# Differential attention in a two-layer decoder trunk: one written order of steps for all compute engines

## The chip, the cores and the metric

The kernel runs on one core of one Trainium2 chip. The core has a matrix engine (TensorE, PE in the profile; its weight loads are shown apart as PEld), a vector engine (VectorE, DVE), a scalar engine for activations (ScalarE, ACT), a general engine (GpSimd, POOL) and a queue engine (SyncE, SP) that starts most DMA transfers. Each engine works through its own list of instructions in order and waits for the others by semaphores. The metric is the device time of one execution in microseconds (us); less is better.

## What is computed

The reference is a trunk of two layers on 512 tokens of width 1024 in float32. Layer 0 runs latent attention (MLA) and differential attention side by side behind one input projection, concatenates the heads and projects back; layer 1 does the same with two other kinds of attention. Behind each layer stands a gated feed-forward block with a short convolution. The part that matters here is the differential attention of layer 0: four heads, each with two queries and two keys of width 64 and a value of width 128.

```
def diff_attention(q1, q2, k1, k2, v, lam, slopes):
    ...
        def probs(qb, kf):
            s = jnp.einsum('bhqd,bhkd->bhqk', qb, kf).astype(jnp.float32) * scale + bias
            return jax.nn.softmax(jnp.where(causal, s, -jnp.inf), axis=-1)

        p = probs(a1, k1) - lam * probs(a2, k2)
        return jnp.einsum('bhqk,bhkd->bhqd', p.astype(v.dtype), v)
...
    o_diff = rms_norm(o_diff, subln_g) * (1.0 - lam_init)
    return jnp.concatenate([heads_last(o_mla), heads_last(o_diff)], axis=-1) @ w_out
```

## The kernel before

Tokens are cut into four row blocks of 128, taken in the order 3, 2, 1, 0 (`ORDER`). Every projection is done with split operands: a weight tile and an activation tile are each held as a high and a low part, and `mm3` makes three matmuls of the pair (high x high, high x low, low x high). Here such a matmul is called a projection step; three of them are one k-tile of 128 rows. Weights arrive by DMA from SP's queue into three raw buffers (`wraw`) and are split by ACT (line 72, the high part `wh`) and DVE (line 73, the low part `wl`) into five pairs of buffers. The class `Weights` keeps the list of units and prepares some (`depth`) ahead of the one that is used.

The stage in question follows MLA. Its work is cut into 16 units, one for each head `h` and row block `i`, of `(i + 1) * 128` keys, since the attention is causal. A unit goes through these functions:

- `score`: two matmuls into two PSUM banks `s` (`sps`, line 844), for z = 0 (q1 k1) and z = 1 (q2 k2); then for each, on DVE, the sum with the ALiBi table and its minimum in one instruction (line 610) and, on ACT, the exponential with its row sum (line 614). DVE then takes the reciprocal of the second row sum (line 855), works out the factor from it, `st1` and `neglam` (line 856), adds the two probability tiles (line 857), and takes the reciprocal of the first row sum (line 858), which scales the output later.
- `turn`: PE transposes the tile block by block (`tpp`, line 621) into the single bank `t`, which ACT (odd row blocks) or DVE (even row blocks) copies out (`pt`, lines 624 and 626).
- `value`: PE multiplies by the value tile `dv` into the single bank `o` (line 869), DVE scales the result (line 871), ACT squares it with a row sum (line 873), POOL makes the inverse root (lines 178 and 181, in `rstd`).
- `norm`: DVE scales the row with that root and the gain `subg` (line 880). `finish`, once a head: four transposes (`tpo`, line 887) and the split into `oD`.

Two kinds of work fill PE in between. `diff_qk` projects queries (`aqk`, evicted by ACT) or keys (evicted by DVE) of heads 1 to 3, eight k-tiles each and six calls in all. `project(i, half, part)` is the output projection of a row block and one half of its columns into `ao`: part 0 takes the MLA outputs (`omh`, `oml`), part 1 those of this stage (`odh`, `odl`), four k-tiles each. `skewed` hands one whole call of these out at every second unit. The eight weight tiles of the output projection (`wout`) come from a small second list `W2` (the first three; two of them are prepared ahead of the units) and from the main list.

PE, ACT, DVE and POOL run in an order that a scheduler works out from this program; `score` asks it for high priority and ties the two scores to the release of both banks (`reads`). Behind the units stands a part whose order is written out by hand (`tc.manual_schedule`): the rest of the output projection, the post-norm, the residual sum and the pre-norm of the feed-forward block, with transposes of the normalised rows (`tp`, line 211). The feed-forward block of layer 0 follows.

Of the kernel before, what the change touches and what calls it, by code (L numbers as in the profile page):

```python
# [17 lines left out]
P = 128  # L18
# [68 lines left out]
def trunk(tc, A, out):  # L87
# [3 lines left out]
    with ExitStack() as top:  # L91
# [498 lines left out]
        def even():  # L590
            with ExitStack() as es:
# [14 lines left out]
                def softmax_negated(sc, ps, table, n, bufs, reads=None):  # L606

                    s = sc.tile([P, S], F32, tag="s", name="s", bufs=bufs)
                    st = sc.tile([P, 2], F32, tag="st", name="st", bufs=6)
# [204 lines left out]
                DVE.tensor_scalar(subg[:], subg[:], 1.0 - LAM_INIT, None, ALU.mult)  # L814
# [13 lines left out]
                wout = [W2.next() for _ in range(2)]  # L828
                nx = new_xnT()

                otoks, dens = {}, {}

                def score(h, i):
                    def f(_):
                        w = (i + 1) * P
                        if i == ORDER[0]:
                            otoks[h] = sc.tile([P, NT, P], F32, tag="otok", name="otok2", bufs=2)
                            dens[h] = sc.tile([P, 6, NT], F32, tag="den", name="den", bufs=2)
                        s_ps = [bank("s", "sps") for _ in range(2)]

                        with tc.high_priority():
                            for z in range(2):
                                r = slice(z * 64, (z + 1) * 64)
                                m = PE.matmul(s_ps[z][:, :w], dq[h][r, i * P:(i + 1) * P], dk[h][r, :w],
                                              start=True, stop=True)
                                if z:
                                    tc.keep_in_program_order(m)
                                else:
                                    for n in reads:
                                        tc.add_manual_dep(m.ins, n, SYNC, reason="both banks")  # L850
                        reads.clear()
                        (s2, st2), (s1, st1) = [softmax_negated(sc, s_ps[z][:, :w], alibi[:, h, 384 - i * P:], w, 5, reads)
                                                for z in (1, 0)]
                        v = dens[h][:, :, i:i + 1]
# [7 lines left out]
                def turn(h, i):  # L862
                    return lambda s: transposed(sc, s, i + 1, i % 2, "t")
# [46 lines left out]
                for h in range(4):  # L910
                    for i in ORDER:
                        st = [score(h, i), turn(h, i), value(h, i), norm(h, i)]
                        if i == ORDER[-1]:
                            st.append(finish(h))
# [508 lines left out]
```

## Time and profile before

| | |
|---|---|
| median of 3 runs | 1164.73 us (1162.73 to 1166.18) |
| the profiled execution | 1163.55 us |
| its span, first to last instruction | 1161.8 us |
| granted TensorE clock, mean | 0.996 |
| instructions | 15175 |
| transferred by DMA | 126.81 MB |

The profile shows one execution. Its page gives the busy time of each engine, a strip of 40 time slices, and groups of instructions by source line. A group says what is written and read by the program's names, the count, the total busy time, the mean of one in ns, and how long the engine was idle ahead of it and for whom. A timeline row gives a start, a duration, engine, line, operation, names, shape and count; `[1.56 <-DVE s L857]` at its end means idle time and who ended it. A window row gives, for a stretch of time, its length and each engine's busy time with the number of instructions, then the granted clock of TensorE, the share of time in which DMA engines were busy, and GB/s. Matmuls of the same engine overlap in the rows, so the pace of PE is read from one start to the next. The float32 matmuls of scores and value products (those without split operands) appear as two records each.

### The profile page before, as it was taken

The numbers are of one execution on the slowest core, as the hardware profiler recorded it, in microseconds if no ns is written. First come the engines' busy times: TensorE is split into PE (matmuls) and PEld (weight loads), VectorE is DVE, ScalarE is ACT, GpSimd is POOL, SyncE is SP. The second block draws the span as 40 slices with busy tenths as digits, with TensorE's granted clock in tenths as the row PEclk, the third lists the DMA queues.
The fourth block names the chain that finished last, engine by engine and source line by source line (L and its number), as shares of the span: only waits on it lengthen the run. The fifth ranks groups of instructions, "written<-read, shape, count | busy, mean of one in ns | idle before, by whom it ended". The sixth has DMA issues, their size and how long they took to land. (4 is left out here: it accounts for less than half of the span.)

```text
span 1161.8 us, 15175 instructions
## 1 busy us (share of the span) xinstructions
PE 1143.3 (98%) x5656; PEld 940.0 (81%) x5656; DVE 810.8 (70%) x1424; ACT 557.9 (48%) x942; POOL 57.0 (5%) x138
## 2 busy tenths in 40 slices
PE   8999999999999999999999999999999999999997
PEld 7876667898888888888888877898988888888885
DVE  6677676467766766899874465577676666679895
ACT  5565555245434434456543454545443443445562
POOL 2100012110000000000030000002000000000001
PEclk9999999999999999999999999999999999999999
DMA  7310521034333332355826213222233333324461
GB/s 278 121 64 1 170 73 37 37 130 128 93 104 93 94 105 84 100 156 162 251 93 177 73 55 93 92 73 94 91 109 96 104 91 97 103 82 145 145 200 73
DMA packets 39049, 126.81 MB, mean 109 GB/s; under 512 B 4672, under 2 KB 6336, under 8 KB 38848
## 3 DMA queue, kind: packets, MB, share of 16 engines
q1 hardware_dynamic: 37056, 122.11, 33.5%
q10 hardware_dynamic: 1920, 3.74, 1.1%
q8 instruction: 44, 0.72, 0.3%
q14 instruction: 29, 0.24, 0.1%
HBM read 117.95 MB, written 6.29 MB: 107 GB/s over the span
## 5 line engine op out<-in xcount | busy, mean ns | idle before, releaser
L73 DVE TENSOR_TENSOR wl<-wraw,wh 128x1024 fp32r<-128x1024 f32 (+1 forms) x202 | 244.4, 1218 | 181.1 <-ACT wh L72 180.9
L72 ACT CAST wh<-wraw 128x1024 fp32r<-128x1024 f32 (+1 forms) x202 | 209.5, 1046 | 282.8 <-PE u L264 179.4
L263 PE MATMUL u<-xh,wh 128*128 128x512 f32 (+1 forms) x768 | 285.0, 372 | 0.9 <-ACT xh L171 0.9
L264 PE MATMUL u<-xl,wh 128*128 128x512 f32 (+1 forms) x768 | 285.2, 372 | 0.1
L265 PE MATMUL u<-xh,wl 128*128 128x512 f32 (+1 forms) x768 | 285.1, 371 | 0.0
L263 PEld LDWEIGHTS u<-xh,wh 128*128 128x128 f32 x768 | 144.5, 188 | 26.3 <-ACT xh L171 1.3
L264 PEld LDWEIGHTS u<-xl,wh 128*128 128x128 f32 x768 | 144.7, 188 | 25.1 <-DVE xl L172 0.3
L265 PEld LDWEIGHTS u<-xh,wl 128*128 128x128 f32 x768 | 144.7, 188 | 24.8
L265 PE MATMUL acc<-wh,gl 128*128 128x512 f32 x248 | 96.5, 389 | 0.0
L264 PE MATMUL acc<-wl,gh 128*128 128x512 f32 x248 | 96.5, 389 | 0.0
L263 PE MATMUL acc<-wh,gh 128*128 128x512 f32 x248 | 96.4, 390 | 0.0
L417 ACT ACTIVATE y<-y 128x512 f32<-128x512 f32 x44 | 27.7, 632 | 85.1 <-DVE y L415 85.1
L412 ACT ACTIVATE y<-u,cw 128x512 f32<-128x512 f32 x88 | 67.4, 773 | 1.7 <-PE u L265 1.7
L415 DVE SCALAR_TENSOR_TENSOR y<-u,cw,y 128x510 f32<-128x510 f32 x88 | 65.6, 747 | 2.5
L413 DVE SCALAR_TENSOR_TENSOR y<-u,cw,y 128x511 f32<-128x511 f32 x88 | 65.1, 743 | 0.9 <-ACT y L412 0.9
L178 POOL TENSOR_TENSOR rv<-ms,epst 128x1 f32<-128x1 f32 x40 | 10.5, 263 | 913.7 <-ACT junk L230 841.4
L263 PEld LDWEIGHTS acc<-wh,gh 128*128 128x128 f32 x248 | 46.6, 188 | 10.2 <-issue 0.6
L265 PEld LDWEIGHTS acc<-wh,gl 128*128 128x128 f32 x248 | 46.6, 188 | 9.8
L264 PEld LDWEIGHTS acc<-wl,gh 128*128 128x128 f32 x248 | 46.6, 188 | 9.5
L263 PE MATMUL apt<-xh,wh 128*128 128x512 f32 x128 | 50.6, 395 | 0.0
L264 PE MATMUL apt<-xl,wh 128*128 128x512 f32 x128 | 50.0, 391 | 0.0
L265 PE MATMUL apt<-xh,wl 128*128 128x512 f32 x128 | 49.9, 390 | 0.0
(298 smaller groups left out, 1905.7 us busy)
## 6 DMA issues: line engine op xcount, KB each, us to landing
wraw<-in_ffn_w_up SPq DMA_DIRECT2D x88, 512.0 KB, 3.6
wraw<-in_ffn_w_down SPq DMA_DIRECT2D x44, 512.0 KB, 3.7
wraw<-in_od_w_dqk SPq DMA_DIRECT2D x12, 512.0 KB, 3.7
wraw<-in_ffn_w_down SPq DMA_DIRECT2D x22, 256.0 KB, 2.7
wraw<-in_ev_w_dqk SPq DMA_DIRECT2D x8, 512.0 KB, 4.0
wraw<-in_ev_w_out SPq DMA_DIRECT2D x8, 512.0 KB, 3.6
spill<-X SPq DMA_DIRECT2D x8, 512.0 KB, 2.6
X<-spill SPq DMA_DIRECT2D x8, 512.0 KB, 6.3
```

The lines of the kernel that those rows point to most:

```text
L72: self.nc.scalar.copy(h[:, :w], raw[:, :w])
L73: self.nc.vector.tensor_tensor(l[:, :w], raw[:, :w], h[:, :w].bitcast(F32), ALU.subtract)
L178: POOL.tensor_tensor(v[:, :n], ms, epst[:, :n], ALU.add)
L263: PE.matmul(o, lh, rh, start=first, stop=False, skip_group_check=more)
L264: PE.matmul(o, lh, rl, start=False, stop=False, skip_group_check=more)
L265: PE.matmul(o, ll, rh, start=False, stop=last, skip_group_check=more)
L412: ACT.activation(y[:, z], u, AF.Identity, bias=c[:, 3:4], scale=c[:, 2:3])
L413: DVE.scalar_tensor_tensor(y[:, z, 1:], u[:, :S - 1], c[:, 1:2], y[:, z, 1:], ALU.mult, ALU.add)
L415: DVE.scalar_tensor_tensor(y[:, z, 2:], u[:, :S - 2], c[:, 0:1], y[:, z, 2:], ALU.mult, ALU.add)
L417: ACT.activation(y[:, 0], y[:, 0], AF.Silu)
```

## The change

The 16 units are no longer handed to `skewed`. A loop over 20 steps, inside `tc.manual_schedule` for PE, DVE, ACT and POOL, writes out which part of which unit comes at which step: the two scores of unit n with their minima; a weight unit prepared (from `W2` at steps 3, 6 and 9); the exponentials of unit n; some filler; the transposes of unit n-1; the value product of unit n-2; more filler; the norm of unit n-3; the combination of unit n; and, every fourth step, `finish`. The filler is now cut into chunks of one k-tile: `plan` gives their number ahead of the transposes and behind the value product, mostly two and two (six projection steps each time). The two halves of row block 1 join the early output projections (`early`). All copies of transposed tiles, and the scaling of the value product, go to ACT. A unit's small columns (minima, sums, reciprocals, row sum of squares) stand in one tile `st` of eight columns; the two reciprocals become one instruction of two columns. The factor of the row mean of squares moves into the gain (`P ** 0.5`) and the epsilon column (`epsp`). No `wout` unit is prepared ahead of the loop, and the main list is prepared by explicit calls inside it (`W.depth` is 0 there), so SP's queue holds the six `ev_w_dqk` loads of heads 1 to 3 ahead of the eight `ev_w_out` loads, where two of the latter stood between.

```diff
@@ -811,7 +812,9 @@
                 ld = sc.tile([P, 1], F32, tag="ld", name="ld")
                 DVE.tensor_tensor(ld[:], le[:, 1:2], le[:, 0:1], ALU.subtract)
                 DVE.tensor_scalar(neglam[:], ld[:], -LAM_INIT, None, ALU.add)
-                DVE.tensor_scalar(subg[:], subg[:], 1.0 - LAM_INIT, None, ALU.mult)
+                DVE.tensor_scalar(subg[:], subg[:], (1.0 - LAM_INIT) * P ** 0.5, None, ALU.mult)
+                epsp = sc.tile([P, 1], F32, tag="epsp", name="epsp")
+                POOL.memset(epsp[:], P * EPS)
...
-                wout = [W2.next() for _ in range(2)]
+                wout = []
                 nx = new_xnT()
 
-                otoks, dens = {}, {}
+                otoks = {}
 
                 def score(h, i):
...
+                    if i == ORDER[0]:
+                        otoks[h] = sc.tile([P, NT, P], F32, tag="otok", name="otok2", bufs=2)
+                    w = (i + 1) * P
+                    ps = [bank("s", "sps")[:, :w] for _ in range(2)]
+                    for z in range(2):
+                        r = slice(z * 64, (z + 1) * 64)
+                        PE.matmul(ps[z], dq[h][r, i * P:(i + 1) * P], dk[h][r, :w], start=True, stop=True)
+                    st = sc.tile([P, 8], F32, tag="st", name="st", bufs=11)
+                    e = [sc.tile([P, S], F32, tag="s", name="s", bufs=5)[:, :w] for _ in range(2)]
+                    for z in range(2):
+                        DVE.tensor_tensor_reduce(out=e[z], in0=ps[z], in1=alibi[:, h, 384 - i * P:], scale=1.0,
+                                                 scalar=3e38, op0=ALU.add, op1=ALU.min, accum_out=st[:, 1 - z:2 - z])
+                    return e, st
+
+                def exps(a):
+                    e, st = a
+                    for z in range(2):
+                        ACT.activation(e[z], e[z], AF.Exp, bias=st[:, 1 - z:2 - z], scale=-1.0,
+                                       accum_out=st[:, 3 - z:4 - z])
+
+                def combine(a):
+                    e, st = a
+                    DVE.reciprocal(st[:, 4:6], st[:, 2:4])
+                    DVE.scalar_tensor_tensor(st[:, 6:7], st[:, 4:5], st[:, 3:4], neglam[:], ALU.mult, ALU.mult)
+                    DVE.scalar_tensor_tensor(e[0], e[1], st[:, 6:7], e[0], ALU.mult, ALU.add)
+                    return e[0], st
 
                 def turn(h, i):
-                    return lambda s: transposed(sc, s, i + 1, i % 2, "t")
+                    return lambda a: (transposed(sc, a[0], i + 1, True, "t"), a[1])
 
                 def value(h, i):
-                    def f(pt):
-                        o = bank("o", "o", P)
+                    def f(a):
+                        pt, st = a
+                        o, otok = bank("o", "o", P), otoks[h]
...
-                        v, otok = dens[h][:, :, i:i + 1], otoks[h]
-                        DVE.tensor_scalar(otok[:, i], o[:], v[:, 2], None, ALU.mult)
+                        ACT.activation(otok[:, i], o[:], AF.Copy, scale=st[:, 5:6])
+
                         jk = sc.tile([P, P], BF16, tag="jk", name="jk")
-                        ACT.activation(jk[:], otok[:, i], AF.Square, scale=P ** -0.5, accum_out=v[:, 3])
-                        return rstd(v[:, 3])
+                        ACT.activation(jk[:], otok[:, i], AF.Square, accum_out=st[:, 7:8])
+                        r = chp.tile([P, 1], F32, tag="rr", name="rr", bufs=4)
+                        POOL.tensor_tensor(st[:, 7:8], st[:, 7:8], epsp[:], ALU.add)
+                        POOL.tensor_tensor(r[:], st[:, 7:8], mhalf[:, 0:1], ALU.pow)
+                        return r
                     return f
 
...
-                def project(i, half, part):
+                def parts_of(i, half, part):
 
                     q = slice(i * P, (i + 1) * P)
+                    c = slice(half * S, half * S + S)
                     if i not in accs:
                         accs[i] = [bank(tag, "ao") for tag in BANK[i]]
                     o = (oM, oD)[part]
                     while len(wout) < 4 * part + 4:
                         wout.append(W.next())
...
-                fillers = [lambda h=h, z=z: diff_qk(h, z) for h in range(1, 4) for z in range(2)]
-                last = fillers.pop()
-                fillers.append(lambda: (last(), wout.append(W2.next())))
-                early = [(i, half) for i in (3, 2) for half in range(2)]
-                fillers += [lambda i=i, half=half: project(i, half, 0) for i, half in early]
-                skewed(units, fillers, 2)
+                    for k in range(4):
+                        wh, wl = wout[4 * part + k]
+                        mm3(accs[i][half], o[0][:, k, q], o[1][:, k, q], wh[:, c], wl[:, c],
+                            part == 0 and k == 0, part == 1 and k == 3)
+                        yield
+
+                def project(i, half, part):
+                    for _ in parts_of(i, half, part):
+                        pass
+
+                def qk_parts(h, z):
+                    acc = bank("a", "aqk")
+                    wh, wl = W.next()
+                    for k in range(KD):
+                        mm3(acc, wh[:, k * P:(k + 1) * P], wl[:, k * P:(k + 1) * P], xh[:, k], xl[:, k],
+                            k == 0, k == KD - 1)
+                        if k < KD - 1:
+                            yield
+                    if z == 0:
+                        ACT.activation(dq[h], acc, AF.Copy, scale=-0.125)
+                    else:
+                        DVE.tensor_copy(dk[h], acc)
+                    yield
+
+                early = [(i, half) for i in (3, 2, 1) for half in range(2)]
+                fills = [qk_parts(h, z) for h in range(1, 4) for z in range(2)]
+                fills += [parts_of(i, half, 0) for i, half in early]
+                busy = []
+
+                def fill(n):
+                    while n and fills:
+                        if not busy:
+                            busy.append(1)
+                        try:
+                            next(fills[0])
+                            n -= 1
+                        except StopIteration:
+                            fills.pop(0)
+                            busy.clear()
+
+                units = [(h, i) for h in range(4) for i in ORDER]
+                scored, turned_, valued = {}, {}, {}
+                plan = ((6, 2),) + ((2, 2),) * 11 + ((2, 1),) * 4 + ((1, 0), (1, 1), (1, 2), (0, 2))
+                depth, W.depth = W.depth, 0
+                with tc.manual_schedule(engines={PE.engine, DVE.engine, ACT.engine, POOL.engine}):
+                    for n in range(len(units) + 4):
+                        if n < len(units):
+                            a = score(*units[n])
+                        if n in (3, 6, 9):
+                            wout.append(W2.next())
+                        elif len(wout) < 4:
+                            W.ahead(min(len(W.made) + 1, W.pos - len(busy) + 5))
+                        if n < len(units):
+                            exps(a)
+                        fill(plan[n][0])
+                        if n >= 1 and n - 1 < len(units):
+                            turned_[n - 1] = turn(*units[n - 1])(scored.pop(n - 1))
+                        if n >= 2 and n - 2 < len(units):
+                            valued[n - 2] = value(*units[n - 2])(turned_.pop(n - 2))
+                        fill(plan[n][1])
+                        if n >= 3 and n - 3 < len(units):
+                            norm(*units[n - 3])(valued.pop(n - 3))
+                        if n < len(units):
+                            scored[n] = combine(a)
+                        if n >= 7 and n % 4 == 3:
+                            finish(n // 4 - 1)(None)
+                    fill(1000)
+                W.depth = depth
                 wout.extend(W.next() for _ in range(4))
```

40 lines of the change are left out of this document (3 added, 37 removed).

## The prediction

> **What bounds the kernel now.** I read the page first, then busy time by windows, then TensorE's waits in the differential-attention stage, then its timeline there.
>
> ```profile
> span 1161.8 us, 15175 instructions
> PE 1143.3 (98%) x5656; PEld 940.0 (81%) x5656; DVE 810.8 (70%) x1424; ACT 557.9 (48%) x942; POOL 57.0 (5%) x138
> ```
>
> ```profile
> 128.00:200.00 72.00, 69.20 (x364) 49.75 (x363) 54.52 (x179) 41.67 (x118) 11.65 (x26) 1.00 0.32 96
> 200.00:240.00 40.00, 39.37 (x187) 32.38 (x186) 16.83 (x26) 12.81 (x32) 7.22 (x22) 1.00 0.10 40
> 240.00:1161.80 921.80, 910.94 (x4513) 763.20 (x4511) 656.12 (x979) 434.09 (x627) 26.60 (x59) 1.00 0.36 112
> ```
>
> The first fence is the head of the page: TensorE (PE) is busy 98% of the span. The second is busy time by stage. Behind 240 us PE stands still for only 921.80 - 910.94 = 10.9 us, the kernel's last tail included, so a microsecond gained ahead of 240 us should arrive at the end nearly whole. In the changed stage (128 to 200 us) VectorE (DVE) works 54.52 and ScalarE (ACT) 41.67 of 72 us: neither is the limit on average, and only when their results come matters.
>
> ```profile
> PE tpp L621 <- DVE s L857: 1.6, 1, 1.6
> PE sps L844 <- DVE st L610: 0.7, 1, 0.7
> PE tpp L621 <- DVE odl L172: 0.6, 1, 0.6
> PE o L869 <- DVE otok L871: 0.4, 2, 0.2
> ```
>
> Here is what PE waited for in the stage: 1.6 + 0.7 + 0.6 + 0.4 = 3.3 us, always for DVE. Waits are not the whole loss, because a busy PE is not PE at its pace. So I price the stage by start-to-start times.
>
> ```profile
> 129.27 0.39 PE L263 MATMUL aqk<-xh,wh 128*128 128x512 f32 x1
> 131.08 0.39 PE L265 MATMUL aqk<-xh,wl 128*128 128x512 f32 x1
> 131.40 0.92 PE L844 MATMUL sps<-dqk 64*128 64x384 f32 x4
> 132.25 0.50 PE L263 MATMUL aqk<-xh,wh 128*128 128x512 f32 x1
> 132.58 0.39 PE L264 MATMUL aqk<-xl,wh 128*128 128x512 f32 x1
> ...
> 223.53 1.04 PE L211 MATMUL tp<-ident,t 128*128 128x128 f32 x8
> ```
>
> These rows run from the first projection step of the stage (129.27) to the first transpose of the normalised rows (223.53): 94.26 us. Between 129.27 and 131.08 lie 8 projection steps, 0.2263 us each. The stage has 144 `aqk` and 120 `ao` steps, 264 x 0.2263 = 59.7 us. The other 34.5 us are the attention's own matmuls, the breaks they make in the projections, and the waits. The break can be read too: the score of 384 columns starts 0.32 us after the step before it, lasts 0.85 us to 132.25, and the step there takes 0.33 us: 0.09 + 0.10 = 0.19 us of break around 0.85 us of work.
>
> ```profile
> 112.91 1.12 PE L844 MATMUL sps<-dqk 64*128 64x512 f32 x2
> 113.96 0.55 PE L744 MATMUL tpp<-ident,s 128*128 128x128 f32 x3
> 114.67 1.12 PE L844 MATMUL sps<-dqk 64*128 64x512 f32 x2
> ...
> 147.35 1.13 PE L844 MATMUL sps<-dqk 64*128 64x512 f32 x4
> 148.41 0.33 PE L621 MATMUL tpp<-ident,s 128*128 128x128 f32 x1
> ...
> 153.40 0.70 PE L844 MATMUL sps<-dqk 64*128 64x256 f32 x4
> 154.03 0.50 PE L263 MATMUL aqk<-xh,wh 128*128 128x512 f32 x1
> ```
>
> Ahead of 129.27 the scheduler had pulled the first unit's two scores (q1 k1 and q2 k2) apart: each alone takes 1.05 us (112.91 to 113.96; the one at 114.67 has the same 1.12 us of busy time), 2.1 us in all. Side by side, as at 147.35, both are through in 1.06 us, and 256 columns take 0.63 us. So before spends 34.5 + 2.1 = **36.6 us** of PE time on the attention outside projections.
>
> **The change, part by part.** PE's instructions are the same in kind and number in this stage; only their order changes, and downstream all engines keep the old order. (a) *Scores.* Four units a head, each standing alone in the projections: 1.06 + 0.85 + 0.63 + 0.42 (0.21 per 128 columns, so the last is an estimate) + 4 breaks x 0.19 = 3.72 us a head. (b) *Transposes and value products*, now one group per step: unit n-1 is transposed right ahead of unit n-2's product.
>
> ```profile
> 157.54 0.60 PE L621 MATMUL tpp<-ident,s 128*128 128x128 f32 x4
> ...
> 158.12 0.47 PE L263 MATMUL aqk<-xh,wh 128*128 128x512 f32 x1
> ...
> 159.59 0.54 PE L621 MATMUL tpp<-ident,s 128*128 128x128 f32 x3
> ...
> 160.78 0.47 PE L263 MATMUL aqk<-xh,wh 128*128 128x512 f32 x1
> ...
> 164.99 0.38 PE L621 MATMUL tpp<-ident,s 128*128 128x128 f32 x2
> ...
> 165.79 0.48 PE L263 MATMUL aqk<-xh,wh 128*128 128x512 f32 x1
> ```
>
> The same pairs stand in the old trace. Four transposes with one product take 0.58 us, three with four 1.19, two with three 0.80; each group has some 0.08 us of break behind it and none ahead. One transpose with two products is not shown; between nothing for the transpose and the 0.80 of the larger pair I take 0.52. Sum: 3.09 + 4 x 0.08 = 3.41 us a head. (c) *Head's end.*
>
> ```profile
> 206.74 0.60 PE L887 MATMUL tpo<-ident,otok 128*128 128x128 f32 x4
> 207.09 0.48 PE L263 MATMUL ao<-wh,odh 128*128 128x512 f32 x1
> ```
>
> Four transposes: 0.35 + 0.09 = 0.44 us. A head costs 3.72 + 3.41 + 0.44 = 7.57 us, four 30.3; the last unit's product, alone, adds 0.3. **Written order: 30.6 us**, if nothing waits: 6.0 us less than before. About 3.3 of it are the listed waits, 0.85 the first unit's scores side by side, the rest short waits and uneven groups. The 40 breaks instead of 30 are in this sum.
>
> (d) *What must arrive in time.* A unit's chain from its first bias-and-minimum on DVE to the combined probabilities:
>
> ```profile
> 148.82 0.68 DVE L610 CUSTOM_DVE_ANT_0 s<-sps,alibi 128x512 f32<-128x512 f32 x1
> ...
> 151.35 0.75 DVE L857 SCALAR_TENSOR_TENSOR s<-s,den 128x512 f32<-128x512 f32 x1
> ```
>
> 148.82 to 151.35 + 0.75 is 3.3 us for the widest unit. The new order puts at least 18 projection steps (4.1 us), the next score (0.85) and the groups of (b) between a score and its transposes: some 6 us, so about 2.5 us are to spare; in the last four steps, with fillers of (2,1), three projection steps or 0.7 us less. Reciprocals merged into one instruction take another 0.16 off DVE's chain; I count nothing for that, since the 2.5 us cover it.
>
> (e) *What changes engine.* The output scaling of 16 units and the copies of the 8 units that DVE evicted go to ACT.
>
> ```profile
> L72 ACT CAST wh<-wraw 128x1024 fp32r<-128x1024 f32 x10 | 10.5, 1046 | 7.4 <-PE aqk L264 4.8 <-DMA wraw<-in_ev_w_out 2.3 <-PE av L265 0.3
> ...
> L624 ACT COPY pt<-tpp 128x256 f32<-128x256 f32 x4 | 1.5, 367 | 0.3 <-PE tpp L621 0.3
> ```
>
> ```profile
> L73 DVE TENSOR_TENSOR wl<-wraw,wh 128x1024 fp32r<-128x1024 f32 x11 | 13.3, 1221 | 3.3 <-ACT wh L72 3.3
> ...
> L871 DVE TENSOR_SCALAR otok<-o,den 128x128 f32<-128x128 f32 x16 | 5.5, 341 | 2.0 <-PE o L869 2.0
> ```
>
> The scaling leaves DVE with 16 x 0.34 = 5.5 us. ACT's price for a 128x128 scaling is not shown: above nothing, below 0.37 us of the 256-column copy; I take 0.34. The copies I take at the 0.37 of that row. ACT gains 24 x 0.36 = 8.5 us on 41.67, so 50 of 72. A step of the new order takes PE 7.57 / 4 + 12 x 0.2263 = 4.6 us, of which ACT at that share uses 3.2: covered. If that cover went, the value product of the next unit, which needs the output bank back, would wait. ACT's order puts each weight cast (L72, 1.05 us) ahead of the step's exponentials; queued behind it are both exponentials, the transposed copy, the scaling and, through them, DVE's combination. Its transfers: the six `ev_w_dqk` loads now stand ahead of the `ev_w_out` loads in SP's queue, where two of the latter stood between. Same bytes, and the loads that PE needs first come first. Bounds: nothing, or the 2.3 us that casts waited on `ev_w_out` in the row above, once; I take nothing, since the first cast so delayed serves a projection 24 steps later.
>
> (f) *The projection of row block 1* (its `omh` half, 8 k-tiles, 24 steps) becomes filler. It leaves less work in front of the first transposes of the normalised rows:
>
> ```profile
> 218.08 0.39 PE L263 MATMUL ao<-wh,omh 128*128 128x512 f32 x1
> ```
>
> ```profile
> 219.79 1.43 DVE L893 SCALAR_TENSOR_TENSOR t<-X,rr,gain 128x512 f32<-128x512 f32 x2
> ```
>
> Projection (2,1) ends near 218.08; normalised halves are ready from 219.79 to 221.22. Before, 24 steps lay between; now 12, or 2.7 us, to 220.8. The first four transposes need the half of 220.5, the rest that of 221.2: from 0 to 0.7 us lost, I take 0.4. The scalings of `subg` and the new `epsp` column are two tiny instructions hidden under the 24 opening projection steps (5.4 us). Other new waits: 0 to 1.0 us (end of (d)); I take 0.3.
>
> **Sum:** 36.6 - 30.6 - 0.4 - 0.3 = 5.3 us off. The profiled execution took 1163.55 us (span 1161.8), so 1158.25; it lay 1.2 us under the median of the three runs, 1164.73, which gives 1159.4. I take 1158.8.
>
> A rule that speaks against the change: the Trainium skill, Perfetto Trace Analysis, section Matmul Optimizations, says that TensorE scales its power with use and that matmuls should run back to back in batches; chunks of two k-tiles make batches of six. By it the stage would lose clock, by the rows below it would not.
>
> ```profile
> 0.00:20.00 20.00, 16.07 (x79) 14.56 (x80) 9.90 (x15) 11.03 (x17) 3.86 (x16) 0.91 0.78 273
> ...
> ```
>
> ```profile
> 133.00:143.00 10.00, 8.44 (x46) 5.99 (x45) 8.20 (x22) 6.55 (x16) 0.00 (x0) 1.00 0.73 224
> ```
>
> The granted clock is 0.91 in the first 20 us, where PE starts, and 1.00 from 133 to 143 us, where PE worked only 8.44 of 10 us. So a hole of 1.6 us cost no clock, and shorter breaks should not.
>
> **Rivals.** *Waits return elsewhere* (20%): a fixed order on four engines stalls all when one is late, where PE's old order was fixed too. For: PE's 3.3 us all waited for DVE, which keeps the weight splits (1.22 us each, L73 above), now at written places between a unit's minima and its combination. Against: the 2.5 us to spare. If waits of the old size come back, 6.0 - 3.3 = 2.7 off: 1160.9.
> *The gain is swallowed at the feed-forward's entry* (5%), the change then doing what it says without effect: its weight casts depend on a transfer. Against: those casts start when PE releases the buffers, so they move with it. 1163.6.
> *Slower: casts hold ACT* (10%). Place: ten weight casts ahead of the exponentials on ACT's queue. From the point where a load lands more than 2.5 us after the step's score, exponentials, combination and transposes are late, and PE, in written order, cannot pass them. The casts did wait for transfers in the old trace (2.3 us). If each of the ten came 3.5 us late, 10 x 1.0 us = 10 lost against 5.3 gained: 1168. Against: at one cast a step and three buffers, a load has two steps, 9 us, to land.
> *Slower: the clock* (3%), as a mechanism of this kernel: short batches lower it to the 0.91 of the start over the 72 us: 72 x (1/0.91 - 1) = 7.1 lost, 1165.4. That is what the page's rule would do.
>
> **How the numbers follow.** Forecast 62%, its own range 1156.5 to 1160.5 (the unknown prices and where the runs lie around the profiled one). To hold eight in ten I go from 1155.5, where no new wait shows, to 1164.0, which takes in the second and third case. Measurements of this kernel tell 0.3% (3.5 us) from no change. Faster: 0.60 of the forecast and 0.08 of the waits case, 0.68. Same: 0.02 + 0.12 + 0.05 and 0.01 of the last two, 0.20. Slower: 0.12.
>
> **What would show it.** Right: PE's waits in the stage fall from 3.3 to under 1 us; the first scores stand together and take 1.06; the first transposes of normalised rows and the feed-forward's first projection come some 5 us earlier, and so does the end. Wrong: PE waits for `s` or `pt` at the transposes or products in many steps (then look at ACT's casts waiting for transfers), a granted clock under 1.00 in the stage, or an early entry to the feed-forward that the end does not show.

## The result, and the profile after

| | before | after |
|---|---|---|
| median, 6 runs each | 1164.43 us (1162.73 to 1166.18) | 1159.6 us (1158.71 to 1161.52) |
| profiled execution | 1163.55 us | 1160.11 us |
| its span | 1161.8 us | 1158.3 us |

The ratio is 0.996, with a 95% interval of 0.995 to 0.9971: faster by 0.4%, or 4.8 us. All six runs of after lie below all six of before, though the interval's weak end, 0.29%, only touches the 0.3% that a measurement of this kernel can tell from no change. The forecast was 1158.8.

The head of the page of after, and its busy time by windows (columns as before: length, PE, PEld, DVE, ACT, POOL, granted clock, DMA share, GB/s):

```profile
span 1158.3 us, 15125 instructions
PE 1142.0 (99%) x5656; PEld 939.6 (81%) x5656; DVE 804.0 (69%) x1384; ACT 566.0 (49%) x966; POOL 57.8 (5%) x139
```

```profile
128.00:200.00 72.00, 71.03 (x367) 51.05 (x366) 46.76 (x142) 46.36 (x133) 10.94 (x26) 1.00 0.29 91
200.00:240.00 40.00, 40.00 (x204) 33.33 (x203) 19.93 (x29) 17.66 (x42) 9.57 (x24) 1.00 0.13 49
```

In the changed stage PE now stands still for 0.97 of 72 us instead of 2.80, DVE has 7.8 us less to do and ACT 4.7 more, and the granted clock is still 1.00.

A single execution's span moves by a microsecond or two for reasons that lie outside the change, so I measure the stage by itself: from the last pair of 512-column scores of MLA to the first projection `u` of the feed-forward block. PE's timeline of before, then of after, at both ends (after also at the first scores and the first transposes of the normalised rows):

```profile
111.95 0.59 PE L726 MATMUL sps<-mk,mq 128*128 128x512 f32 x1
...
241.66 0.28 PE L263 MATMUL u<-xh,wh 128*128 128x256 f32 x1
```

```profile
112.19 0.59 PE L727 MATMUL sps<-mk,mq 128*128 128x512 f32 x1
...
127.27 1.13 PE L843 MATMUL sps<-dqk 64*128 64x512 f32 x4
128.33 0.50 PE L263 MATMUL aqk<-xh,wh 128*128 128x512 f32 x1
...
222.24 0.60 PE L211 MATMUL tp<-ident,t 128*128 128x128 f32 x4
...
237.76 0.28 PE L263 MATMUL u<-xh,wh 128*128 128x256 f32 x1
```

The stage takes 241.66 - 111.95 = 129.71 us before and 237.76 - 112.19 = 125.57 after: **4.14 us off**. It began 0.24 us later and what follows it took 1158.3 - 237.76 = 920.54 us against 920.14, so the span shows 3.5. Over all runs below the stage began between 110.44 and 112.94 us, though PE's order up to there is the same in all, and the rest took 920.0 to 921.9: that is the noise that the stage's length is free of (the last section shows where a part of it comes from). Each stage length is still that of one execution.

Of PE's waits in the stage one is left (first fence: PE's waits there, with total, times and longest; second: the row where it happens):

```profile
PE tpp L622 <- DVE s L861: 1.0, 1, 1.0
```

```profile
183.10 0.41 PE L622 MATMUL tpp<-ident,s 128*128 128x128 f32 x2 [0.97 <-DVE s L861]
```

These are the transposes of unit 10, waiting for its combination (line 861). DVE's timeline of after in the 3 us before it:

```profile
180.16 0.69 DVE L934 COPY dqk<-aqk 128x512 f32<-128x512 f32 x1 [2.29 <-PE aqk L265]
180.76 0.34 DVE L886 SCALAR_TENSOR_TENSOR otok<-otok,rr,subg 128x128 f32<-128x128 f32 x1
181.03 0.16 DVE L859 RECIPROCAL st<-st 128x2 f32<-128x2 f32 x1
181.10 1.20 DVE L73 TENSOR_TENSOR wl<-wraw,wh 128x1024 fp32r<-128x1024 f32 x1
182.22 0.21 DVE L860 SCALAR_TENSOR_TENSOR st<-st,neglam 128x1 f32<-128x1 f32 x1
182.47 0.48 DVE L861 SCALAR_TENSOR_TENSOR s<-s,st 128x256 f32<-128x256 f32 x1
```

Two things stand ahead of the combination. DVE idles 2.29 us because the next instruction in its order is the eviction of the keys (line 934), and that projection ends only with step 10's second filler. Then, between the unit's reciprocal and its factor, comes a weight split of 1.20 us (line 73). The loop doesn't issue it: it belongs to the weight unit taken by the call behind the loop, and the scheduler put it there. Before, the largest wait had the same shape. DVE's timeline of before, ahead of its 1.6 us wait at 137.52:

```profile
135.49 1.23 DVE L73 TENSOR_TENSOR wl<-wraw,wh 128x1024 fp32r<-128x1024 f32 x1 [1.08 <-ACT wh L72]
136.63 0.75 DVE L857 SCALAR_TENSOR_TENSOR s<-s,den 128x512 f32<-128x512 f32 x1
```

There too the combination of a unit stood behind a weight split on DVE, and the split behind its cast on ACT.

### The profile page after: what moved, and what is told of

The parts are those of the page before. It is cut to its first block, busy times and chain, and to the rows that moved or that the text cites. A ratio compares the mean times of both kernels' runs of the same rounds, so it can differ in the third digit from the quotient of the medians.

```text
span 1158.3 us, 15125 instructions
## 1 busy us (share of the span) xinstructions
PE 1142.0 (99%) x5656; PEld 939.6 (81%) x5656; DVE 804.0 (69%) x1384; ACT 566.0 (49%) x966; POOL 57.8 (5%) x139
```

## The experiments

All stage lengths are read as above: 129.71 us before, 125.57 with the change. Edits are against the changed kernel unless something else is said.

### What makes the one wait that is left

**The weight unit inside the loop.**

```diff
-                        elif len(wout) < 4:
+                        elif len(wout) < 4 or n == 12:
```

> The last weight unit of the output projection that the loop leaves out is prepared inside it, at step 12, so that its split on DVE no longer stands between the reciprocal and the factor of unit 10. I read the stage from the last pair of 512-column MLA scores to the first projection of the feed-forward block: 129.71 us before, 125.57 with the change. Theory (the inserted split makes the one wait of 1.0 us at the transposes of unit 10): the wait is gone, stage 124.6, span 1157.3. Rival (the key eviction ahead of the unit's normalisation makes it late anyway): the wait stays at 0.5 to 1.0 us, stage 125.1 to 125.6.

Stage 124.56 us (-1.01), no wait of PE in it; median 1158.49, ratio to before 0.9954 (0.9939 to 0.9969). The theory holds, by its number: without the split the key eviction alone costs PE nothing that the profile lists.

**The combination ahead of the second filler.**

```diff
+                        if n < len(units):
+                            scored[n] = combine(a)
                         fill(plan[n][1])
...
-                        if n < len(units):
-                            scored[n] = combine(a)
```

> The combination of a unit is written ahead of the step's second filler instead of behind it, so that on DVE it stands ahead of the key eviction that the filler ends with at steps 2, 6 and 10. Theory (the late key eviction is what takes the slack at these three steps): the waits at 163 us (0.13) and 183 us (1.0) go, stage 124.5 us against 125.57. Rival (the inserted weight split alone makes the wait): the split now stands ahead of another combination, the wait moves by one step and keeps 0.5 to 1.0 us, stage 125.1 to 125.6.

Stage 124.22 us (-1.35), no wait; median 1158.36, ratio 0.9953 (0.9935 to 0.997). DVE's timeline of this run, at unit 10:

```profile
177.04 0.16 DVE L859 RECIPROCAL st<-st 128x2 f32<-128x2 f32 x1
177.24 0.22 DVE L860 SCALAR_TENSOR_TENSOR st<-st,neglam 128x1 f32<-128x1 f32 x1
177.49 0.48 DVE L861 SCALAR_TENSOR_TENSOR s<-s,st 128x256 f32<-128x256 f32 x1
179.42 0.69 DVE L934 COPY dqk<-aqk 128x512 f32<-128x512 f32 x1 [1.44 <-PE aqk L265]
```

The combination is through at 177.97; with the change it ended at 182.95, about 5 us later, and the stage began only 0.56 us later there. The split now stands ahead of another combination and does no harm. So it takes both, the late eviction and the split behind it: the eviction alone made no wait in the run with the weight unit inside the loop, and the split ahead of another combination, at 180.70, makes none here. Either edit removes the wait, and this one gives the slack back at all three steps with an eviction.

**The scheduler decides.** The loop stays, but nothing binds the engines to its order.

```diff
-                with tc.manual_schedule(engines={PE.engine, DVE.engine, ACT.engine, POOL.engine}):
+                with ExitStack():
```

> The loop stays as it is written, but the scheduler decides the order of the engines instead of being bound to it. PE's order in the stage is then the same up to the last four steps, where transposes, products and the remaining fillers stand in another order, and in layer 1 a group of projections moves. Theory (the gain comes from the order of the statements, not from its being fixed): stage within 0.7 us of the 125.57 with the change. Rival (the fixed order is what avoids the waits): 2 to 4 us of waits come back, stage 127.5 to 129.5.

Stage 124.78 us (-0.79), no wait; median 1157.93, ratio 0.9945 (0.993 to 0.996). The rival is out: fixing the order buys nothing. DVE's timeline of this run shows that the scheduler itself puts the combination ahead of the eviction:

```profile
179.53 0.48 DVE L861 SCALAR_TENSOR_TENSOR s<-s,st 128x256 f32<-128x256 f32 x1
...
181.31 0.68 DVE L934 COPY dqk<-aqk 128x512 f32<-128x512 f32 x1
```

### How much slack the chains have

**Two more passes on DVE in every unit's chain.**

```diff
                     e, st = a
+                    for _ in range(2):
+                        DVE.tensor_scalar(e[1], e[1], 1.0, None, ALU.mult)
                     DVE.reciprocal(st[:, 4:6], st[:, 2:4])
```

> Two more passes over one probability tile, each a multiplication by 1.0 (some 0.48 us for 512 columns, less for narrower units), stand on DVE ahead of every unit's reciprocals, so every chain from score to transposes gets up to 0.96 us longer; the result is the same. Theory (about 2.5 us to spare at most steps, none at steps 2, 6 and 10, where a key eviction stands ahead): those three lose up to 1 us each, the others nothing: 2 to 3 us more, stage 127.6 to 128.6. Rival (the chain is everywhere at its limit): 4 x (0.96 + 0.8 + 0.6 + 0.45) = 11 us more, stage 136.8.

Stage 127.03 us, +1.46. PE's waits, and one pair of passes on DVE (x2):

```profile
PE tpp L622 <- DVE s L863: 2.2, 3, 1.5
```

```profile
169.42 0.88 DVE L860 TENSOR_SCALAR s<-s 128x512 f32<-128x512 f32 x2
```

The three waits are at 143.77 (0.24), 162.64 (0.50) and 182.97 us (1.51): units 2, 6 and 10, and no other. The 13 other chains took up to 0.8 us more (169.42 to the reciprocal at 170.22) and PE did not notice. The theory named the places; its size was a little high.

### Which part of the change brings the gain

**Whole projections again.** The written order, with eight k-tiles at every second step in place of four in each.

```diff
-                plan = ((6, 2),) + ((2, 2),) * 11 + ((2, 1),) * 4 + ((1, 0), (1, 1), (1, 2), (0, 2))
+                plan = ((8, 0), (8, 0), (0, 0), (8, 0)) + ((0, 0), (8, 0)) * 4 + ((0, 0), (4, 0)) * 2 + ((1, 0), (1, 1), (1, 2), (0, 2))
```

> The written order with whole projections: eight k-tiles at a time at every second step from step 1 on (and 8, 4, 4 at steps 11, 13, 15), ahead of the transposes, in place of chunks of two. Theory (what counts is that the order is written so that something long stands ahead of each group; the size of a chunk matters little, and score breaks cost 0.19 us each wherever they stand): stage 124.0 to 125.6. Rival (the small chunks, two in each step, are what keeps the chains covered): the steps without filler wait 0.3 to 0.6 us each, 8 of them, 2.4 to 4.8 us more: 127 to 129.

Stage 129.57 us, +4.0; 1163.54 in its one run. The theory falls: with this plan the written order keeps nothing of the gain. PE's waits in the stage:

```profile
PE tpp L622 <- DVE s L861: 2.4, 3, 0.8
PE tpp L622 <- DVE odl L172: 0.9, 2, 0.6
PE tpp L622 <- ACT otok L873: 0.2, 1, 0.2
```

But the waits are fewer and longer than the rival had them, and they make 2.5 us of the 4.0 (3.5 less the 1.0 that the change has anyway). The rest stands in PE's rows without being listed: the two scores at 172.87, for instance, take 1.35 us to the next step, where such a pair takes 0.85 with the change. DVE's timeline ahead of the first:

```profile
140.29 0.69 DVE L934 COPY dqk<-aqk 128x512 f32<-128x512 f32 x1 [4.64 <-PE aqk L265]
...
141.34 0.62 DVE L861 SCALAR_TENSOR_TENSOR s<-s,st 128x384 f32<-128x384 f32 x1
```

It is the key eviction again: DVE idles 4.64 us for it, and the combination written behind it comes when PE has nothing left in front of the next transposes. The 0.9 us stand behind the split of a finished head (line 172), as the 0.6 us of before did. So what the small chunks do is to leave filler behind the point where a late DVE instruction comes free. Whether whole projections would do as well with the combination written first was not tried.

**Scaling and copies back on DVE.**

```diff
-                    return lambda a: (transposed(sc, a[0], i + 1, True, "t"), a[1])
+                    return lambda a: (transposed(sc, a[0], i + 1, i % 2, "t"), a[1])
...
-                        ACT.activation(otok[:, i], o[:], AF.Copy, scale=st[:, 5:6])
+                        DVE.tensor_scalar(otok[:, i], o[:], st[:, 5:6], None, ALU.mult)
```

> The scaling of the value products and the copies of transposed tiles of even row blocks go back to DVE, in the written order. Theory (DVE and ACT both have slack, the move between them is worth little): 0 to 2 us more, stage 125.6 to 127.6, the 1.0 us wait at unit 10 a little longer. Rival (the move to ACT is what took PE's waits for DVE away): the waits of before come back, 2.5 to 3.3 us more, stage 128 to 129.

Stage 125.50 us (-0.07), the same single wait of 1.0 us; median 1159.77, ratio 0.9961 (0.9947 to 0.9975). The move between engines is worth nothing. The scaling's group in this run and in the changed kernel:

```profile
L873 DVE TENSOR_SCALAR otok<-o,st 128x128 f32<-128x128 f32 x16 | 5.6, 349 | 6.9 <-PE o L872 6.9
```

```profile
L873 ACT ACTIVATE otok<-o,st 128x128 f32<-128x128 f32 x16 | 5.9, 368 | 2.3 <-PE o L872 2.1
```

It costs 0.35 us on the one and 0.37 on the other, and PE waits for neither.

**Row block 1 put back.**

```diff
-                early = [(i, half) for i in (3, 2, 1) for half in range(2)]
+                early = [(i, half) for i in (3, 2) for half in range(2)]
```

> The projection of row block 1 from the MLA outputs goes back behind the units, as before the change. The filler then runs out in the last six steps. Theory (24 steps of filler are what covers the chains of the last units): PE waits for the last units' tiles, up to 3 to 5 us, less 0.3 us of the wait of the first normalised rows (PE tp for DVE t), which goes: stage 128 to 131. Rival (the last units don't need it, the chain fits in what stands there anyway): the 0.3 us goes and nothing comes, stage 125.2.

Stage 131.86 us, +6.3; 1165.85 in its one run, 1.4 us above the median of before and within the scatter of its runs. More than expected, and in one place, PE's timeline of this run:

```profile
204.06 0.49 PE L872 MATMUL o<-dv,pt 128*128 128x128 f32 x2
206.92 0.66 PE L893 MATMUL tpo<-ident,otok 128*128 128x128 f32 x4 [2.38 <-DVE otok L886]
208.26 0.79 PE L263 MATMUL ao<-wh,odh 128*128 128x512 f32 x1 [0.67 <-ACT odh L171]
```

The filler has run out, and from the last value product PE waits through scaling, square, root and norm to the head's transposes, and then for their split: 208.26 - 204.06 = 4.2 us with 0.5 us of matmuls in it. With the breaks that is 4.0 us more than the same matmuls cost with the change. The rest came behind it, in a way that neither theory had. Busy time and granted clock (the number after POOL's) in the same stretch:

```profile
205.00:206.00 1.00, 0.00 (x0) 0.00 (x0) 0.35 (x1) 0.38 (x2) 0.79 (x3) 1.00 0.00 0
206.00:207.00 1.00, 0.08 (x1) 0.11 (x2) 0.35 (x1) 0.00 (x0) 0.39 (x1) 1.00 0.00 0
...
208.00:209.00 1.00, 0.74 (x2) 0.52 (x3) 0.69 (x1) 0.20 (x1) 0.00 (x0) 0.50 0.00 0
209.00:214.00 5.00, 5.00 (x14) 3.93 (x13) 0.69 (x1) 0.69 (x2) 0.19 (x1) 0.50 0.00 0
```

From the second hole on the clock is halved until about 214 us. In the window from 209 to 214 only about 12 projection steps start, 0.43 us apart instead of 0.23: over the 13 steps or so that are slow, some 2.5 us more. In this execution the hole was paid for twice; the last section shows that a hole need not be.

**The same, with the filler shared out for it.**

```diff
-                plan = ((6, 2),) + ((2, 2),) * 11 + ((2, 1),) * 4 + ((1, 0), (1, 1), (1, 2), (0, 2))
+                plan = ((6, 2),) + ((2, 2),) * 10 + ((2, 0),) * 5 + ((1, 0), (1, 1), (0, 2), (0, 1))
```

> As the run that put the projection of row block 1 back (131.86 us), but the remaining filler is shared out for it: four k-tiles a step up to step 10 (the queries and keys must be ready), two a step ahead of the transposes in steps 11 to 15, and six left for the last four. Theory (the 6.3 us of that run came from a plan that ran out of filler ahead of the last head's end, not from the 24 steps as such): the 3.7 us hole at the last head's end shrinks to under 1, short waits at steps 12 to 15 of 0 to 0.5 us each come instead: stage 126.5 to 129. Rival (without those 24 steps the chains can't be covered whatever the sharing): 130 to 132.

Stage 126.07 us, only 0.50 above the changed kernel, a little better than the theory had it; 1160.38 in its one run. The waits are the one at unit 10 and 0.3 us at a head's end behind it. So the 24 steps as such are worth half a microsecond; what must not happen is that the plan has none left at the end.

**Before, with row block 1 early.** `early` is set to `(3, 2, 1)` as in the change, on the kernel before.

> The kernel before, with the projection of row block 1 from the MLA outputs added to the early ones and nothing else changed; the 24 projection steps come behind the last head's end and before the rest. Theory (this part alone is worth little in the old order, where other projections cover the last head's end already): the 0.6 us wait at 202 us stays, since the filler comes behind it, the first normalised rows lose 0.3 as with the change: stage 129.5 to 130.2 against 129.71. Rival (this is the part that brings the gain): 3 to 6 us off, 124 to 127.

Median 1164.43 us, ratio 1.0001 (0.9992 to 1.001): no effect. Stage 130.48, 0.77 above before and 0.3 above the theory's range. PE's waits in its stage are those of before (1.7, 0.8 of the 1.2, 0.6 and 0.4) and 0.4 us more at the scores (`sps` for DVE `st`).

### What a score and its break cost

**The two scores apart.** One of the filler chunks moves between them; the plan's first numbers are one less.

```diff
+                        if z == 0:
+                            fill(1)
```

> One filler chunk of three projection steps is moved between the two scores of every unit, as the scheduler had done to the first unit of the kernel before; instructions are the same in number. Theory (two scores on opposite halves of the array run side by side when they stand together, and every break costs 0.19 us): each of the 16 units pays its score twice, (1.06 + 0.85 + 0.63 + 0.42) x 4 = 11.8 us, and one break more, 16 x 0.19 = 3.0: 14.9 us more, stage 140.4. Rival (a pair costs twice the single score anyway and the 1.06 us are the price of both in turn): only the breaks, 3.0 us more, stage 128.6.

Stage 139.57 us, +14.0; 1174.01 in its one run. PE's timeline of this run, at the first unit:

```profile
125.77 1.12 PE L843 MATMUL sps<-dqk 64*128 64x512 f32 x2
126.83 0.50 PE L263 MATMUL aqk<-xh,wh 128*128 128x512 f32 x1
...
127.72 1.12 PE L843 MATMUL sps<-dqk 64*128 64x512 f32 x2
128.77 0.50 PE L263 MATMUL aqk<-xh,wh 128*128 128x512 f32 x1
```

Each single score takes the 1.06 and 1.05 us that both take when they stand together (127.27 to 128.33 with the change). The wait at unit 10 shrank to 0.35 us here, which is 0.6 of the 0.9 that the theory is off. So the first unit's two scores, torn apart before, did cost one score more.

**All filler in one piece.**

```diff
-                plan = ((6, 2),) + ((2, 2),) * 11 + ((2, 1),) * 4 + ((1, 0), (1, 1), (1, 2), (0, 2))
+                plan = ((8, 0),) + ((4, 0),) * 11 + ((3, 0),) * 4 + ((1, 0), (1, 1), (1, 2), (0, 2))
```

> All filler of a step stands in one piece between the score and the transposes, (4, 0) in place of (2, 2): as many projection steps, but the value products run into the next score, so 16 breaks fewer. Theory (a break costs 0.19 us by its count): 16 x 0.19 = 3.0 us off the stage, 122.5 us. Rival (a score that follows a product pays its own break all the same, as the four head's-end transposes followed by a score cost 1.70 = 0.45 + 1.25 us; only the pace of the longer piece gets better): 0.6 to 1.0 us off, 124.6 to 125.0. Either way the unit's chain gets 6 more projection steps of slack, so the 1.0 us wait at unit 10 goes as well, a further 1.0 us; the value product now waits for its transposed tile with less between.

Stage 124.41 us (-1.16), no wait; median 1158.52, ratio 0.995 (0.9935 to 0.9964). Without the wait's 1.0 only some 0.2 us are left for the breaks that fell away (PE's rows have 20 in place of 35, so 15 and not 16). The theory falls, and the rival had even too much. PE's timeline of this run shows why:

```profile
145.84 0.38 PE L622 MATMUL tpp<-ident,s 128*128 128x128 f32 x2
146.06 0.83 PE L872 MATMUL o<-dv,pt 128*128 128x128 f32 x6
146.82 1.13 PE L843 MATMUL sps<-dqk 64*128 64x512 f32 x4
147.88 0.50 PE L263 MATMUL aqk<-xh,wh 128*128 128x512 f32 x1
```

From 145.84 to 147.88 are 2.04 us, with 0.11 behind 2.15: the price of two transposes with three products alone (0.89) and of a score alone (1.25, both in the table below) add up to 2.14. A score pays its break whatever stands ahead of it.

### The three cures together

> Three edits that each took the 1.0 us wait away, together: the last weight unit inside the loop, the combination ahead of the key eviction, and all filler of a step in one piece. Theory (they remove the same wait and hardly anything else; breaks are not saved): stage 124.1 to 124.5, median 1158.0 to 1158.6. Rival (their savings add up): 122.6 and 1156.8.

Stage 124.32 us; median 1158.76, ratio 0.9957 (0.9943 to 0.997). They remove the same wait and don't add up. No variant without the wait (medians 1157.93 to 1158.76) is told apart from another by its runs, and their intervals overlap that of the change (0.995 to 0.9971): the microsecond is shown by the traces, five times, not by the times alone. The shortest edit that gets it is the one line that prepares the weight unit in the loop.

## Why the prediction was right, and where its working was not

The time came within a microsecond of the forecast. The terms did less well than the sum: 5.3 us were forecast off the stage and its profile shows 4.1, while the medians of the runs lie 4.8 apart, a difference of the size by which single executions scatter. So it is in part luck that the time came out this near.

The working's own measure, made again: from the first score (127.27) to the first transpose of the normalised rows (222.24) are 94.97 us, with 12 more projection steps in it than before (276, since row block 1's first half is filler now). Without 276 x 0.2263 = 62.5 us, **32.5 us** are left, where the prediction had 30.6 + 0.4 + 0.3 = 31.3, and before 36.6.

- *Prices (a) to (c)* held. Start-to-start prices with the breaks around them, from PE's timeline of after:

| group | predicted | measured |
|---|---|---|
| score of 512, 384, 256, 128 columns | 1.25, 1.04, 0.82, 0.61 | 1.25, 1.05, 0.84, 0.64 |
| 4 transposes + 1 product, 3 + 4, 2 + 3, 1 + 2 | 0.66, 1.27, 0.88, 0.60 | 0.67, 1.23, 0.89, 0.57 |
| head's end; last product | 0.44; 0.3 | 0.45; 0.26 |

  All groups of the stage add up to 31.73 us, 30.66 without the wait at unit 10 and its restart (1.07): 30.6 was predicted.
- *The step that failed is (d), "so about 2.5 us are to spare".* I took the chain's own length against what PE has in front of the transposes, for a unit like any other, and 0.3 us for all new waits. At steps 2, 6 and 10 DVE can't start the combination when the exponentials are done, since a key eviction that ends with the second filler is written ahead of it; there the slack is 0.3 us or less, as the run with the two passes showed (waits at these units alone). The split set in at unit 10 made it 1.07 us, and the run that moved the split removed it. That this split would stand there could be read from the order of the changed kernel's instructions; the working took DVE's order only by the chain's own length.
- *The other 0.8 us* (32.5 - 30.7 - 1.1) are in the projection's pace. I priced every step at the 0.2263 us of the long opening stretch. Behind a break the pace is lower, in PE's timeline of after:

```profile
131.43 0.39 PE L264 MATMUL aqk<-xl,wh 128*128 128x512 f32 x1
...
133.69 0.39 PE L265 MATMUL aqk<-xh,wl 128*128 128x512 f32 x1
...
148.43 0.50 PE L263 MATMUL aqk<-xh,wh 128*128 128x512 f32 x1
...
149.93 0.27 PE L622 MATMUL tpp<-ident,s 128*128 128x128 f32 x1
```

  In the opening stretch 10 steps take 2.26 us. The chunk of six behind the score at 148.43 takes 1.50 us to 149.93, or 1.40 without the 0.10 that is already in the break: 0.233 a step. In before's sum such a loss (0.5 us, by the steps that have a step on either side) was inside the 36.6 that I read off, so it was taken from one side only.
- *(e)* held: the scaling costs ACT 0.368 us (0.34 taken), and with it on DVE nothing changes. The casts did not hold ACT up: their waits for transfers from 128 to 200 us fell from 2.9 us (2.3 for `wh`, 0.6 for `wo`) to a single one of 1.1.
- *(f)*: 0.4 us taken, and nearly nothing lost: PE's waits show none at the first transposes of the normalised rows, and from 222.24 to `u` the changed kernel takes 15.5 us, against 241.66 - 223.53 less 12 steps, 15.4. (The wait of 0.3 us for `t` on which two of the expectations counted stands at 247.88, behind `u`, and did not go with row block 1.)
- *What would show it*: the first scores together at 1.06 us, as predicted; the entry to the feed-forward 3.9 us earlier by the clock of the two profiles, not 5; one wait of 1.0 us, at the edge of what I had given. The first transposes of the normalised rows came only 1.3 us earlier (222.24 against 223.53), not some 5: this sign forgot that by (f) 12 more projection steps, 2.7 us, now stand ahead of them.
- *The rivals*: waits did return, by the mechanism named (a DVE instruction at a written place between a unit's minima and its combination), but 1 us and not 3. The clock stayed at 1.00 from 128 to 240 us with 35 breaks up to the first transposes of the normalised rows (PE's rows of before have 26 there, so my 40 instead of 30 were miscounted; the sum doesn't use them). So the rule of the Trainium skill that was weighed there (Perfetto Trace Analysis, Matmul Optimizations) would have sent the forecast the wrong way: breaks of 0.2 us cost no clock. But my reading of the 0.91 in the first 20 us, "where PE starts", was wrong: the clock is full up to 13 us and is halved behind a wait of PE. The last section shows how far that goes.

What brings the gain? Not the binding of the engines, the move to ACT or row block 1, each of which could be undone for 0.5 us or less, if the filler is shared out. About 1 us is the first unit's pair of scores; 2.3 us are listed waits that went (3.3 to 1.0); the remaining 0.8 is not taken apart further. The order of the loads, the merged reciprocals and the moved factors were not undone by themselves, so their share is not known. Even sharing of the filler keeps the waits away: with whole projections, and the combination where the change has it, the gain is gone.

## What to carry to other kernels

When an order is written out by hand, follow each engine's queue through one whole period and look for the instruction that waits for the *end* of something (an eviction) and stands ahead of one that others wait for; put the second first, or leave filler behind it. Instructions that are issued outside the written block can still be set into it, ahead of a link of the critical chain. And price a long uniform stretch by its pace in short pieces when the change cuts it up.

## What the runs showed of the hardware

**Behind a hole of some 2 us in PE's work the clock was halved for some microseconds, but not each time.** In the run with row block 1 put back PE idles for 2.4 us up to 206.92 and for 0.7 more up to 208.26, and the clock is at 0.50 from 208 until 214. In the first 20 us of before PE waits 2.0 us for `xh` up to 10.97 and 0.6 more up to 12.19. Busy time and clock of before, in and behind these waits:

```profile
9.00:10.00 1.00, 0.00 (x0) 0.00 (x0) 0.95 (x1) 0.70 (x1) 0.00 (x0) 1.00 1.06 432
...
13.00:14.00 1.00, 1.00 (x4) 0.96 (x4) 1.00 (x2) 1.00 (x2) 0.00 (x0) 0.54 0.79 318
```

The clock is still full in the hole and drops only some 2 us behind its end; it is full again from 17 us on. The same wait, of 1.9 to 2.5 us, stands in all fourteen traces of this case, and in ten of them the clock is halved behind it. In the other four it stays at 1.00, with waits of 2.0 to 2.4 us (the two more passes, the two scores apart, the filler shared out, before with row block 1 early). In two of these four it is halved later, at 662 and 649 us, behind a listed wait of only 0.8 us that before and after have too, without a drop. PE's timeline and the windows of the run with the two scores apart:

```profile
11.06 0.46 PE L263 MATMUL ac<-wh,xh 128*128 128x416 f32 x1 [2.37 <-ACT xh L171]
```

```profile
13.00:14.00 1.00, 1.00 (x6) 0.99 (x7) 1.00 (x2) 1.00 (x2) 0.00 (x0) 1.00 0.78 312
...
663.00:664.00 1.00, 1.00 (x4) 0.81 (x3) 1.00 (x3) 0.21 (x1) 0.00 (x0) 0.50 0.73 291
```

So the length of one hole does not settle whether the clock drops, and these runs leave open what does. The holes of 1.6 us (before, 137.52) and 1.5 us (the run with two more passes, 182.97) stood without a drop. The Trainium skill (TensorE: Matmul & The Clock Gate, Why this matters for your kernels) advises against idle gaps above some 3 us between bursts of matmuls, for this reason; in ten of these traces a gap of about 2 us, with a shorter one behind it, was enough.

This is also a part of the noise between executions. In the four traces without the early drop the stage begins at 110.4 to 110.7 us, in the ten others at 111.1 to 112.9; and the two with the late drop have the longest rest, 921.9 us each. Apart from the run with row block 1 put back, no trace has a drop inside the stage.

**The break of a score is its own.** A score of 64 rows in float32 pays its 0.19 us whether projections or value products stand ahead of it: all groups of the stage cost 30.7 us without the wait in the changed kernel and 30.2 in the run with 15 breaks fewer, where 15 x 0.19 = 2.9 us would have gone if a break were paid by its count.

**Projection steps behind a break are slower for a while**: means of 0.232 to 0.233 us for the second to fourth step and 0.2269 from the thirteenth on, over the stage of the changed kernel.
